# Shared weight buffers in the first group of an FFN's down product, a query rotation issued in pieces, an early output projection over two heads, and statistics and a gate chain queued later

## The chip, the core and the metric

The kernel runs on one core of a Trainium2 chip. A core has a matrix engine (TensorE, PE in the profile, with its weight loads shown apart as PEld), a vector engine (DVE), a scalar engine (ACT), GpSimd (POOL, here mostly a queue that issues transfers) and SyncE (SP, the queue that issues the weight loads). The metric is device time in microseconds, the median over runs.

## The reference

One decoder trunk on x (1024 positions, 1024 channels), all in fp32: a convolution layer, an FFN, an attention layer, an FFN and a last norm.

```python
h = h + short_conv_mixer(rms_norm(h, g))    # u = h @ w_in (1024 x 3072); b, c, val = split(u)
                                            # z = c * val; conv of width 3 over z; (b * conv) @ w_out
h = h + swiglu_ffn(rms_norm(h, g))          # g, u = split(h @ w13), 2 x 2816; (silu(g) * u) @ w2
c_lat, k_pe = ...                           # hn @ w_dkv: latent of 256, 64 rotated columns; k_nope, v = c_lat @ w_ukv
h = h + mla_mixer(rms_norm(h, g))           # query latent of 384, 8 heads of 128 + 64 rotated columns, causal softmax,
                                            # all heads with the same rotated key; then @ w_o (1024 x 1024)
h = h + swiglu_ffn(rms_norm(h, g))
return rms_norm(h, final_norm_g)
```

The rotation is `[x1*cos - x2*sin, x1*sin + x2*cos]` of the 64 rotated columns of a query head.

## The kernel before

Everything is held transposed: channels on the 128 partitions, the 1024 positions in the free dimension. Every fp32 operand of a product is split into a high and a low part (`split`, two instructions: ACT writes the high part at L92, DVE the low part at L93), and a product is three matmuls: high by high, high by low, low by high.

**Products by seven.** A product over pairs of blocks, two 128-row blocks of output by two halves of the positions, is done with seven products instead of eight (`pair`, L148 on, and `blocks`). For each it needs sums and differences of weight blocks (`sums`, L159 to L165, on DVE) and of operands (`mixed` in `operands`). The seven go in the order of `SEQ`. The results land in PSUM banks `ps_z` and `ps_y`, and a hook copies or adds them up. `raw_blocks` loads the four weight blocks of a pair of output rows into raw buffers named w11, w12, w22, w21 (pool `wraw`, ten buffers of 128x512), one more buffer holds the sums. The split weights go to five buffers `wo`.

**An FFN.** `up` runs over 22 blocks j of the inner width and leaves two at a time as the operands of one *pair* kp (11 pairs). `operands` builds seven split operands per pair (`xm`), which `move` (L85, POOL's queue) writes to memory (`md`), but for the last pair (kp 10), which stays on chip (`kept`). `back` then does the down product in groups of pairs given by `GROUPS`: in each group it runs over the four pairs of output rows, and adds to `h`. In the first group a pair is loaded with `load` after the third last `up`, the other after the last. While one group runs, the operands of the next are loaded. A group of kp 10, 2, 3 is not contiguous in the weights, so its four blocks take two transfers each.

**Attention.** For each head `scores` makes eight blocks of softmax (max at L946 on DVE, exponent at L949 on ACT), `pv` transposes them (`pt`) and multiplies by V; heads 0 to 5 go to memory (`od`), heads 6 and 7 stay on chip. `jobs` holds what is placed between: K and query of the next head, and, for two heads at once, the rotated query (`make_qr`) and V. `make_qr` rotates with `rope` (four DVE operations of 1024 positions), splits, and moves the eight quarters into place (`qrs`) on POOL's queue. In the last head the output projection of heads 0 and 1 (`project_o`, eight jobs) fills in; its operands (`oth`, `otl`) and the stream `h` come over POOL's queue.

**Convolution layer.** The first three products are done the plain way (`classic`), the rest by seven; `mix_x` queues the 16 mixed operands that these need. `gate_value` queues the gate chain (`scaled`, `taps`, `last`).

**What sets the order.** `queue` holds pieces of vector work that `drip` issues one at a time after each product. The text order is not the order on the engines: a list scheduler with a simulated timeline sets each engine's instruction order when the program is built, and the buffers of the pools are given out in the order of allocation. An instruction that writes a buffer waits for the last reader of what was there before.

Of the kernel before, what the change touches and what calls it, by code (L numbers as in the profile page):

```python
# [24 lines left out]
H = 8  # L25
# [11 lines left out]
EARLY = 2  # L37
GROUPS = ((0, 1), (10, 2, 3), (4, 5, 6), (7, 8, 9))
PREFETCH = 4
# [15 lines left out]
def trunk(ctx, tc, aps, out):  # L55
# [74 lines left out]
    def raw_blocks(w, kps, c1, c2):  # L130

        nk = len(kps)
        wv = w.rearrange("(k h p) n -> p h k n", p=P, h=2)
        R = {}
        for kh, c, key in ((0, c1, "11"), (0, c2, "12"), (1, c2, "22"), (1, c1, "21")):
            t = wraw("w" + key)
            i = 0
            while i < nk:
                n = 1
                while i + n < nk and kps[i + n] == kps[i] + n:  # L140
                    n += 1
                nc.sync.dma_start(t[:, i * P:(i + n) * P].rearrange("p (k m) -> p k m", m=P),
                                  wv[:, kh, kps[i]:kps[i] + n, c:c + P])
                i += n
            R[key] = t
        return R
# [332 lines left out]
    def back(w, load, st, final, ready, kept):  # L479
# [3 lines left out]
        for gi, g in enumerate(GROUPS):  # L483
            todo = []
            if gi + 1 < len(GROUPS):
                nxt = GROUPS[gi + 1]
                new = [{} for _ in nxt]
                if gi == 0:
                    new[0] = kept
                todo = [(i, kp, name) for name in SEQ for i, kp in enumerate(nxt) if gi or i]  # L490
            pace = -(-(NSLOT - KD - 2 - 7 * (len(g) + (gi == 0))) // 3)
# [43 lines left out]
    def next_operands(st, gain, spill=True):  # L535
# [3 lines left out]
        def final(mp):  # L539
            xs = []  # L540
            for n in (2 * mp, 2 * mp + 1):
                if spill:
                    move(hd[n], st[n])
                x = slot("xg")
                nc.scalar.activation(x, st[n], AF.Copy, scale=gcol(gain, n))
                xs.append(x)
            X.append({})
            operands(*xs, X[mp].__setitem__)
            for n in (2 * mp, 2 * mp + 1):
                queue.append(lambda n=n: stats(n, st[n]))  # L550
            if mp == KD // 2 - 1:
                drip()
        return X, final
# [7 lines left out]
    def first_product(w, c1, c2, emit):  # L561

        if run["n"] == 1:
            mix_x()
        if run["n"] < CLASSIC:
# [37 lines left out]
    def gate_value(j):  # L603
# [83 lines left out]
    def ffn(w13, w2, X, after, side=None):  # L687
# [35 lines left out]
        ready, kept = [{} for _ in GROUPS[0]], {}  # L723
        for j in range(KF):
            up(j)
            if j % 2:
                put = kept.__setitem__ if j == KF - 1 else lambda name, o, j=j: move(md[j // 2, SEQ.index(name)], o)
                operands(mid.pop(j - 1), mid.pop(j), put)
            if side:
                queue.append(lambda: next(side, None))  # L730
            if j == KF - 3:
                for name in SEQ:
# [34 lines left out]
    def rope(dst, src):  # L767

        t = slot("rt")
        nc.vector.tensor_tensor(t[0:64], src[64:128], sinT[64:128], ALU.mult)  # L770
# [59 lines left out]
    def rotated_keys():  # L830
        kr = slot("kr")
        rope(kr, kr0)
        nc.vector.tensor_tensor(kr, kr, get_R(), ALU.mult)
# [75 lines left out]
    def make_qr(h):  # L909
# [13 lines left out]
        nc.scalar.copy(out=q0, in_=ps)  # L923
        rope(qr, q0)
        yh, yl = slot("qrh", F32R), slot("qrl", F32R)
        split(yh, yl, qr)
        for a in range(2):
            t = slot("qrs", F32R)
            for i, y in enumerate((yh, yl)):
                for q in range(2):  # L930
                    r = i * 64 + q * 32
                    move(t[r:r + 32], y[q * 64 + a * 32:q * 64 + a * 32 + 32])
            Qt.setdefault(h + a, {})["r"] = t

# [57 lines left out]

    make_k(0)
    make_qr(0)
    make_q(0)
    make_v(0)
# [34 lines left out]
    for h in range(H):  # L1031
        if h >= 6:
            Od[h] = (slot("oth", F32R), slot("otl", F32R))
        if h + 1 < H:
# [9 lines left out]
        per = {2: ((0,), (1,), (), ()) if h == 0 else ((), (0,), (1,), ()), 4: ((0,), (1,), (2,), (3,)), 8: ((0, 1), (2, 3), (4, 5), (6, 7))}[len(jobs)]  # L1044
# [119 lines left out]
```

## Time and profile before

| | before |
| --- | --- |
| median of 3 runs | 2158.4 us (2157.68 to 2165.13) |
| profiled execution | 2161.49 us |
| its span | 2159.7 us |
| mean granted PE clock | 0.987 |
| PE busy | 2090.6 us, 97% |
| DVE busy | 1631.9 us, 76% |
| ACT busy | 938.7 us, 43% |
| DMA, mean rate | 149 GB/s |

How to read the rows below: a row of a timeline gives the start, the length, the engine, the line, the operation, output and input tiles, sizes, and in brackets the time the engine sat idle ahead of it and what ended that. A row of waits gives what waited, for what, the total in us, how many times, and the longest. A row of windows gives for one stretch the busy time of PE, PEld, DVE, ACT and POOL with the number of instructions, then the clock granted to PE, the DMA engines' busy share, and GB/s. In the stages of the kernel, the convolution layer runs to about 366 us, the first FFN to about 1000, attention from there to about 1490 with its heads between 1108 and 1440, and the second FFN to the end; `down` starts at about 790 and 1917.

### The profile page before, as it was taken

To read this page: it belongs to the slowest core of one execution; us is meant where nothing else is said; L and a number is where in the kernel's file an instruction comes from. 1 tells how busy PE (TensorE), PEld (TensorE's weight loads), DVE (VectorE), ACT (ScalarE), POOL (GpSimd) and SP (SyncE) were. 2 spreads that over 40 slices of the span, in tenths; PEclk is the share of its full clock that TensorE was granted. 3 is DMA by queue.
4 is the path that set the end of the run, shared out by engine and by line. 5 is a ranking of instruction groups with operands and counts; after the bars stand their busy time and mean duration, and the time that the engine had idled before them with its cause. 6 is when DMAs were issued, how large, how long until landed. Compare 5 with 4: busy or idle time off the path is not lost.

```text
span 2159.7 us, 27697 instructions
## 1 busy us (share of the span) xinstructions
PE 2090.6 (97%) x9798; PEld 1739.5 (81%) x9798; DVE 1631.9 (76%) x2694; ACT 938.7 (43%) x1729; POOL 244.0 (11%) x464
## 2 busy tenths in 40 slices
PE   8999999999999999999999999899999999999998
PEld 6788887888888877778888888787888888877886
DVE  5787757789988876689467777568888888876785
ACT  6533344444444443224345445345444444442235
POOL 1000100001101121110011112100001010121100
PEclk9999999999999999999999999999999999999998
DMA  6033462344545685865222213522435454685851
GB/s 242 25 98 119 143 206 93 122 142 129 183 130 177 206 286 195 272 214 163 51 57 60 55 42 85 199 80 78 132 122 176 145 162 147 192 275 195 282 190 78
DMA packets 267371, 321.29 MB, mean 149 GB/s; under 512 B 19855, under 2 KB 214608, under 8 KB 267232
## 3 DMA queue, kind: packets, MB, share of 16 engines
q0 software_dynamic: 61248, 201.46, 27.6%
q1 hardware_dynamic: 205984, 118.07, 18.5%
q8 instruction: 77, 1.26, 0.2%
q14 instruction: 62, 0.51, 0.1%
HBM read 206.22 MB, written 108.00 MB: 145 GB/s over the span
## 4 chain that ended last, share of the span: by engine, by line
PE 87%; DVE 6%; DMA 3%; ACT 2%; issue 2%; SPq 0%; POOL 0%; POOLq 0%; DVEq 0%; ACTq 0%
PE ps_z L184 36%; PE ps_y L184 27%; PE ps_c L229 6%; PE ps_s L943 3%; DMA w<-in_conv_ffn_w_dram 1%; PE ps_wo L105 1%; PE ps_wo L107 1%; PE ps_wo L109 1%; PE ps_l L109 1%; PE ps_l L105 1%; PE ps_l L107 1%; DMA w<-in_mla_ffn_w_dram 1%; PE ps_q L105 1%; PE ps_q L109 1%; PE ps_q L107 1%
## 5 line engine op out<-in xcount | busy, mean ns | idle before, releaser
L184 PE MATMUL ps_z<-x,wo 128*128 128x512 f32 x2532 | 612.6, 391 | 16.3 <-ACT z L198 6.9
L184 PEld LDWEIGHTS ps_z<-x,wo 128*128 128x128 f32 x2532 | 476.5, 189 | 118.7 <-ACT z L198 8.3
L184 PE MATMUL ps_y<-x,wo 128*128 128x512 f32 x1764 | 432.1, 390 | 1.2 <-DVE x L93 0.9
L184 PEld LDWEIGHTS ps_y<-x,wo 128*128 128x128 f32 x1764 | 330.8, 188 | 71.3 <-DVE x L93 2.1
L92 ACT CAST wo<-w 128x512 fp32r<-128x512 f32 (+2 forms) x423 | 239.4, 571 | 271.9 <-PE ps_y L184 109.2
L93 DVE TENSOR_TENSOR wo<-w,wo 128x512 fp32r<-128x512 f32 (+2 forms) x423 | 261.9, 625 | 58.7 <-ACT wo L92 58.1
L184 PE MATMUL ps_z<-xm,wo 128*128 128x512 f32 x960 | 242.9, 396 | 6.7 <-ACT wo L92 3.9
L184 PEld LDWEIGHTS ps_z<-xm,wo 128*128 128x128 f32 x960 | 181.5, 191 | 48.4 <-ACT wo L92 5.0
L92 ACT CAST wo<-sums 128x512 fp32r<-128x512 f32 (+2 forms) x172 | 98.7, 574 | 274.0 <-PE ps_y L184 102.1
L184 PE MATMUL ps_y<-xm,wo 128*128 128x512 f32 x720 | 185.2, 394 | 1.5 <-DVE h L504 1.3
L184 PEld LDWEIGHTS ps_y<-xm,wo 128*128 128x128 f32 x720 | 136.7, 191 | 32.4 <-DVE h L504 2.8
L85 POOL DMA_DIRECT2D md<-x x140 | 75.1, 537 | 740.0 <-DVE x L93 707.2
L198 ACT COPY z<-ps_z 128x512 f32<-128x512 f32 x106 | 62.2, 587 | 140.7 <-PE ps_z L184 140.5
L93 DVE TENSOR_TENSOR wo<-sums,wo 128x512 fp32r<-128x512 f32 (+2 forms) x172 | 107.9, 627 | 12.4 <-ACT wo L92 10.9
L504 DVE TENSOR_TENSOR h<-ps_z,h 128x512 f32<-128x512 f32 x104 | 71.7, 689 | 44.4 <-PE ps_z L184 43.6
L85 POOL DMA_DIRECT2D xm<-md x140 | 74.4, 538 | 266.9 <-PE ps_z L184 131.2
L93 DVE TENSOR_TENSOR x<-t,x 128x512 fp32r<-128x512 f32 x136 | 92.6, 689 | 3.3 <-ACT x L92 3.1
L238 DVE TENSOR_TENSOR a<-ps_y,z 128x512 f32<-128x512 f32 x88 | 60.8, 691 | 44.2 <-PE ps_y L184 43.9
L92 ACT CAST x<-t 128x512 fp32r<-128x512 f32 x136 | 83.0, 622 | 23.0 <-DVE t L253 20.1
L949 ACT ACTIVATE p<-ps_s,mx,qscale 128x128 f32<-128x128 f32 (+3 forms) x64 | 53.4, 836 | 79.9 <-DVE mx L947 79.9
L159 DVE TENSOR_TENSOR sums<-w,w 128x512 f32<-128x512 f32 (+2 forms) x85 | 53.4, 628 | 34.6 <-DMA w<-in_mla_ffn_w_dram 15.1
L504 DVE TENSOR_TENSOR h<-ps_y,h 128x512 f32<-128x512 f32 x88 | 60.5, 688 | 22.5 <-PE ps_y L184 22.4
(296 smaller groups left out, 3357.4 us busy)
## 6 DMA issues: line engine op xcount, KB each, us to landing
md<-x POOLq DMA_DIRECT2D x140, 512.0 KB, 3.7
xm<-md POOLq DMA_DIRECT2D x140, 512.0 KB, 8.4
w<-in_conv_ffn_w_dram SPq DMA_DIRECT2D x88, 256.0 KB, 2.9
w<-in_mla_ffn_w_dram SPq DMA_DIRECT2D x88, 256.0 KB, 3.0
w<-in_conv_w_in_dram SPq DMA_DIRECT2D x48, 256.0 KB, 2.9
hd<-h POOLq DMA_DIRECT2D x24, 512.0 KB, 3.6
hs<-hd SPq DMA_DIRECT2D x16, 512.0 KB, 12.0
yd<-yb POOLq DMA_DIRECT2D x12, 512.0 KB, 3.4
```

Source lines behind the costliest of these rows:

```text
L85: nc.gpsimd.dma_start(dst, src)
L92: nc.scalar.copy(out=hi, in_=src)
L93: (eng or nc.vector).tensor_tensor(lo, src, hi.bitcast(F32), ALU.subtract)
L105: nc.tensor.matmul(ps[:, hs], lhsT=wh, rhs=xh(k)[:, hs], start=st, stop=False)
L107: nc.tensor.matmul(ps[:, hs], lhsT=wh, rhs=xl(k)[:, hs], start=False, stop=False)
L109: nc.tensor.matmul(ps[:, hs], lhsT=wl, rhs=xh(k)[:, hs], start=False, stop=en)
L184: mm = lambda w_, x_, f: nc.tensor.matmul(b, lhsT=w_[:, m], rhs=x_, start=f, stop=True, skip_group_check=True)
L198: nc.scalar.copy(out=kept[name], in_=b)
L229: nc.tensor.matmul(ps[:, ts], lhsT=w_[:, m], rhs=X[i][f"b{kh}{th}"][:, q, :], start=st and j == 0, stop=en and j == 2)
L238: nc.vector.tensor_tensor(dst, ps, add, ALU.add)
L504: nc.vector.tensor_tensor(dst[name], b, dst[name], ALU.add)
L943: nc.tensor.matmul(ps[:, a:b], lhsT=q[:, qs], rhs=k[:, a:b], start=i == 0, stop=i == 4 and b < kw)
```

## The change

Five edits.

1. **Down's first group.** The groups of pairs are now (0, 1), (2, 3, 4), (5, 6, 7), (8, 9, 10). The pair kept on chip is kp 4, whose `up` blocks are computed last. Where a group has two pairs, w11 and w12 share one raw buffer, and so do w22 and w21. Every block is one transfer.
2. **The rotation** returns its four operations as pieces, which `make_qr` queues, followed by the split and the moves; one piece is issued after each block of scores.
3. **The early projection** is spread: three jobs in head 6 and five in head 7, at the places in `PLACES`. The operands of heads 0 and 1 and the first of `h` are loaded at the start of head 6.
4. **The gate chain**: `mix_x` is called after the first product of `gate_value(0)`, ahead of the chain of the first gate value in the queue.
5. **The statistics** of the last two blocks of `h` stay in the queue after the last operands of an FFN are issued.

```diff
-GROUPS = ((0, 1), (10, 2, 3), (4, 5, 6), (7, 8, 9))
+GROUPS = ((0, 1), (2, 3, 4), (5, 6, 7), (8, 9, 10))
+KEPT = 4
+PLACES = {0: ((0,), (1,), (), ()), 6: ((0,), (1,), (2, 3), (4,)), 7: ((0,), (1, 2), (3,), (4,))}
+PLACES.update({h: ((0,), (1,), (2,), (3,)) if h % 2 else ((), (0,), (1,), ()) for h in range(1, 6)})
@@ raw_blocks
-        for kh, c, key in ((0, c1, "11"), (0, c2, "12"), (1, c2, "22"), (1, c1, "21")):
-            t = wraw("w" + key)
-            i = 0
-            while i < nk:
...
-                nc.sync.dma_start(t[:, i * P:(i + n) * P].rearrange("p (k m) -> p k m", m=P),
-                                  wv[:, kh, kps[i]:kps[i] + n, c:c + P])
-                i += n
+        for q, (kh, c, key) in enumerate(((0, c1, "11"), (0, c2, "12"), (1, c2, "22"), (1, c1, "21"))):
+            if nk > 2 or q % 2 == 0:
+                t = wraw("w" + key)
+            else:
+                t = t[:, HS // 2:]
+            nc.sync.dma_start(t[:, :nk * P].rearrange("p (k m) -> p k m", m=P), wv[:, kh, kps[0]:kps[0] + nk, c:c + P])
@@ back
-                if gi == 0:
-                    new[0] = kept
-                todo = [(i, kp, name) for name in SEQ for i, kp in enumerate(nxt) if gi or i]
+                if KEPT in nxt:
+                    new[nxt.index(KEPT)] = kept
+                todo = [(i, kp, name) for name in SEQ for i, kp in enumerate(nxt) if kp != KEPT]
@@ next_operands
             if mp == KD // 2 - 1:
-                drip()
+                drip(len(queue) - 2)
@@ first_product
-        if run["n"] == 1:
-            mix_x()
@@ gate_value
         if j == 0:
+            mix_x()
             x_stats()
@@ ffn
-        for j in range(KF):
+        order = [k for kp in range(KF // 2) if kp != KEPT for k in (2 * kp, 2 * kp + 1)] + [2 * KEPT, 2 * KEPT + 1]
+        for j in order:
...
-            if j == KF - 3:
+            if j == order[-3]:
@@ rope
-        nc.vector.tensor_tensor(t[0:64], src[64:128], sinT[64:128], ALU.mult)
-        nc.vector.tensor_tensor(t[64:128], src[0:64], sinT[0:64], ALU.mult)
-        nc.vector.tensor_tensor(dst, src, cosT, ALU.mult)
-        nc.vector.tensor_tensor(dst, dst, t, ALU.add)
+        tt = nc.vector.tensor_tensor
+        return [lambda: tt(t[0:64], src[64:128], sinT[64:128], ALU.mult),
...
+                lambda: tt(dst, dst, t, ALU.add)]
@@ make_qr
-        rope(qr, q0)
+        def done():
...
+        queue.extend(rope(qr, q0))
+        queue.append(done)
@@ the loop over heads
-        else:
+        if h == H - 2:
             O0 = [load_o(k) for k in range(EARLY)]
-            for n in range(4):
+        if h == H - 1:
+            for n in range(3, 5):
                 h_of(n)
             O1 = [load_o(k) for k in range(EARLY, 6)] + [Od[6], Od[7]]
-            jobs = [lambda n=n: project_o(O0, 0, n) for n in range(KD)]
+        if h >= H - 2:
+            early = range(KD)[:3] if h == H - 2 else range(KD)[3:]
+            for n in early[:2]:
+                h_of(n)
+            jobs += [lambda n=n: project_o(O0, 0, n) for n in early]
+        per = PLACES[h]
         for i in range(4):
             pa, pb = p_tiles(i)
-            scores(Kt[h], Qt[h], 2 * i, pa)
-            scores(Kt[h], Qt[h], 2 * i + 1, pb)
+            if i == 0:
+                drip()
+            for qb, p in ((2 * i, pa), (2 * i + 1, pb)):
+                scores(Kt[h], Qt[h], qb, p)
+                drip(1)
```

What this does to the engines' order, at three places. First SP's queue, where the first FFN's `down` begins (w11 to w21 are raw buffers, a number for each allocation; `w2` is down's weight). Before:

```order
L142 DMA w11_6272<-in_conv_ffn_w2_dram 128x2x128
L142 DMA w12_6274<-in_conv_ffn_w2_dram 128x2x128
L142 DMA w22_6276<-in_conv_ffn_w2_dram 128x2x128
L142 DMA w21_6278<-in_conv_ffn_w2_dram 128x2x128
L142 DMA w11_6393<-in_conv_ffn_w2_dram 128x2x128
L142 DMA w12_6395<-in_conv_ffn_w2_dram 128x2x128
```

And now:

```order
L143 DMA w11_6272<-in_conv_ffn_w2_dram 128x2x128 x2
L143 DMA w22_6275<-in_conv_ffn_w2_dram 128x2x128 x2
L143 DMA w11_6391<-in_conv_ffn_w2_dram 128x2x128 x2
L143 DMA w22_6394<-in_conv_ffn_w2_dram 128x2x128 x2
L143 DMA w11_6492<-in_conv_ffn_w2_dram 128x2x128 x2
```

The same loads in the same order, into two allocations for a pair of output rows where there were four.

Second DVE in head 1, where the rotated query of heads 2 and 3 is made (`rt` and `qr` are the rotation, `mx` the maximum of a block of scores, `oh` and `pt` what PE waits for). Before:

```order
L770 TENSOR_TENSOR rt<-q_9227,sinT 64x1024
L771 TENSOR_TENSOR rt<-q_9227,sinT 64x1024
L772 TENSOR_TENSOR qr<-q_9227,cosT 128x1024
L946 TENSOR_REDUCE mx<-ps_s_9249 128x1
L93 TENSOR_TENSOR pt<-ps_t,pt 128x128
L946 TENSOR_REDUCE mx<-ps_s_9263 128x1
L773 TENSOR_TENSOR qr<-qr,rt 128x1024
L947 TENSOR_SCALAR mx<-mx,nqscale 128x1 x2
L93 TENSOR_TENSOR wqr<-wqr 128x2x2x32 x3
L93 TENSOR_TENSOR oh<-ps_pv,oh 128x256
L93 TENSOR_TENSOR qrl<-qr,qrh 128x1024
```

And now, first the two halves of `rt`, later in the head the rest:

```order
L770 TENSOR_TENSOR rt<-q_9203,sinT 64x1024
L771 TENSOR_TENSOR rt<-q_9203,sinT 64x1024
L954 RECIPROCAL rsum<-rsum 128x1
L950 TENSOR_REDUCE mx<-ps_s_9222 128x1
L955 TENSOR_SCALAR p<-p,rsum 128x384
L96 TENSOR_TENSOR oh<-ps_pv,oh 128x256
```

```order
L772 TENSOR_TENSOR qr<-q_9203,cosT 128x1024
L950 TENSOR_REDUCE mx<-ps_s 128x1
L954 RECIPROCAL rsum<-rsum 128x1
L773 TENSOR_TENSOR qr<-qr,rt 128x1024
L951 TENSOR_SCALAR mx<-mx,nqscale 128x1
L955 TENSOR_SCALAR p<-p,rsum 128x640
```

The product with the cosine and the sum now stand among the maxima of the fifth and sixth block of scores; the low half of the split (`qrl`) follows the maximum of the eighth.

Third POOL's queue at heads 6 and 7 (`od` takes the heads' output to memory, `oth` and `otl` bring it back, `h<-hd` loads the stream). Before:

```order
L85 DMA od<-oh 128x256 x10
L85 DMA oth<-od 128x1024
L85 DMA otl<-od 128x1024
L85 DMA oth<-od 128x1024
L85 DMA otl<-od 128x1024
L85 DMA h<-hd 128x1024 x4
L85 DMA oth<-od 128x1024
```

And now:

```order
L88 DMA od<-oh 128x256
L88 DMA oth<-od 128x1024
L88 DMA otl<-od 128x1024
L88 DMA oth<-od 128x1024
L88 DMA otl<-od 128x1024
L88 DMA h<-hd 128x1024 x2
L88 DMA od<-oh 128x256 x6
L88 DMA h<-hd 128x1024 x3
L88 DMA oth<-od 128x1024
```

The loads for the early projection and two blocks of `h` stand ahead of the last six moves of the heads' output.

More of the change, by code (lines that the diff above doesn't have):

```diff
@@ L134, in raw_blocks @@
         R = {}
-        for kh, c, key in ((0, c1, "11"), (0, c2, "12"), (1, c2, "22"), (1, c1, "21")):
-            t = wraw("w" + key)
-            i = 0
-            while i < nk:
[L139 to L142, printed above, removed]
-                                  wv[:, kh, kps[i]:kps[i] + n, c:c + P])
-                i += n
+        for q, (kh, c, key) in enumerate(((0, c1, "11"), (0, c2, "12"), (1, c2, "22"), (1, c1, "21"))):
[4 more added lines that the diff above has]
+            nc.sync.dma_start(t[:, :nk * P].rearrange("p (k m) -> p k m", m=P), wv[:, kh, kps[0]:kps[0] + nk, c:c + P])
             R[key] = t
@@ L723, in ffn @@
         ready, kept = [{} for _ in GROUPS[0]], {}
-        for j in range(KF):
+        order = [k for kp in range(KF // 2) if kp != KEPT for k in (2 * kp, 2 * kp + 1)] + [2 * KEPT, 2 * KEPT + 1]
+        for j in order:
             up(j)
             if j % 2:
-                put = kept.__setitem__ if j == KF - 1 else lambda name, o, j=j: move(md[j // 2, SEQ.index(name)], o)
+                put = kept.__setitem__ if j // 2 == KEPT else lambda name, o, j=j: move(md[j // 2, SEQ.index(name)], o)
                 operands(mid.pop(j - 1), mid.pop(j), put)
@@ L769, in rope @@
         t = slot("rt")
-        nc.vector.tensor_tensor(t[0:64], src[64:128], sinT[64:128], ALU.mult)
-        nc.vector.tensor_tensor(t[64:128], src[0:64], sinT[0:64], ALU.mult)
-        nc.vector.tensor_tensor(dst, src, cosT, ALU.mult)
-        nc.vector.tensor_tensor(dst, dst, t, ALU.add)
+        tt = nc.vector.tensor_tensor
+        return [lambda: tt(t[0:64], src[64:128], sinT[64:128], ALU.mult),
+                lambda: tt(t[64:128], src[0:64], sinT[0:64], ALU.mult),
+                lambda: tt(dst, src, cosT, ALU.mult),
+                lambda: tt(dst, dst, t, ALU.add)]
     w_dkv = A["w_dkv"].rearrange("(k p) n -> p k n", p=P)
@@ L831, in rotated_keys @@
         kr = slot("kr")
-        rope(kr, kr0)
+        for f in rope(kr, kr0):
+            f()
         nc.vector.tensor_tensor(kr, kr, get_R(), ALU.mult)
@@ L923, in make_qr @@
         nc.scalar.copy(out=q0, in_=ps)
-        rope(qr, q0)
[L925 to L933, printed above, removed]
+        def done():
+            yh, yl = slot("qrh", F32R), slot("qrl", F32R)
+            split(yh, yl, qr)
+            for a in range(2):
+                t = slot("qrs", F32R)
+                for i, y in enumerate((yh, yl)):
+                    for q in range(2):
+                        r = i * 64 + q * 32
+                        move(t[r:r + 32], y[q * 64 + a * 32:q * 64 + a * 32 + 32])
+                Qt.setdefault(h + a, {})["r"] = t
+        queue.extend(rope(qr, q0))
+        queue.append(done)
     def scores(K, Q, qb, p):
@@ L1033, in trunk @@
             Od[h] = (slot("oth", F32R), slot("otl", F32R))
+        jobs = []
         if h + 1 < H:
@@ L1037, in trunk @@
                 jobs = [lambda: make_qr(h + 1), lambda: make_v(h + 1)] + jobs
-        else:
+        if h == H - 2:
             O0 = [load_o(k) for k in range(EARLY)]
-            for n in range(4):
+        if h == H - 1:
+            for n in range(3, 5):
                 h_of(n)
             O1 = [load_o(k) for k in range(EARLY, 6)] + [Od[6], Od[7]]
-            jobs = [lambda n=n: project_o(O0, 0, n) for n in range(KD)]
-        per = {2: ((0,), (1,), (), ()) if h == 0 else ((), (0,), (1,), ()), 4: ((0,), (1,), (2,), (3,)), 8: ((0, 1), (2, 3), (4, 5), (6, 7))}[len(jobs)]
+        if h >= H - 2:
[4 more added lines that the diff above has]
+        per = PLACES[h]
         for i in range(4):
             pa, pb = p_tiles(i)
-            scores(Kt[h], Qt[h], 2 * i, pa)
-            scores(Kt[h], Qt[h], 2 * i + 1, pb)
+            if i == 0:
+                drip()
+            for qb, p in ((2 * i, pa), (2 * i + 1, pb)):
+                scores(Kt[h], Qt[h], qb, p)
+                drip(1)
             if len(pend) == DEPTH:
```

## The prediction

> **What bounds the kernel now.** I read the page's busy times and its chain by engine first, then PE's waits, then the windows in which they fall, then the timelines around the longest of them.
>
> ```profile
> PE 2090.6 (97%) x9798; PEld 1739.5 (81%) x9798; DVE 1631.9 (76%) x2694; ACT 938.7 (43%) x1729; POOL 244.0 (11%) x464
> PE 87%; DVE 6%; DMA 3%; ACT 2%; issue 2%; SPq 0%; POOL 0%; POOLq 0%; DVEq 0%; ACTq 0%
> ```
>
> PE is busy for 2090.6 of 2159.7 us and makes 87% of the chain that ended last. It is the bound, and the change adds and removes no matmul. So it can gain only PE's idle time (69.1 us) and matmuls that ran slowly. PE's waits, as total, times, longest:
>
> ```profile
> PE ps_z L184 <- DVE wo L93: 7.9, 4, 4.4
> PE ps_z L184 <- ACT z L198: 6.9, 3, 2.6
> PE ps_t L969 <- DVE oh L93: 4.6, 6, 1.2
> PE ps_z L184 <- ACT wo L92: 4.2, 3, 2.4
> ...
> PE ps_pv L981 <- ACT pt L92: 3.5, 1, 3.5
> ...
> PE ps_pv L981 <- DVE pt L93: 3.0, 3, 1.0
> PE ps_s L943 <- ACT p L949: 2.4, 2, 2.1
> PE ps_s L943 <- DVE h L1020: 2.1, 1, 2.1
> ```
>
> These eight are 34.6 us and are what the edits touch: `wo` is the split weight operand of a product (part A below), `oh` and `pt` with DVE stand in the heads that rotate a query (B), ACT `pt`, `p` and DVE `h` where the heads meet the output projection (C), `z` beside the gate chain and the changes of stage (D). The windows (PE, PEld, DVE, ACT, POOL busy; granted clock; DMA share; GB/s) price the rest of a gap:
>
> ```profile
> 756.00:810.00 54.00, 50.62 (x214) 40.50 (x213) 42.86 (x78) 25.26 (x50) 13.80 (x26) 0.97 0.84 286
> 810.00:864.00 54.00, 49.59 (x210) 40.53 (x209) 34.12 (x67) 17.73 (x37) 7.43 (x14) 0.94 0.60 195
> 1350.00:1404.00 54.00, 47.81 (x257) 41.33 (x258) 32.13 (x67) 18.04 (x41) 5.83 (x11) 0.91 0.55 198
> 1836.00:1890.00 54.00, 54.00 (x240) 44.72 (x239) 45.04 (x68) 24.96 (x42) 8.06 (x16) 1.00 0.60 190
> 1890.00:1944.00 54.00, 50.24 (x210) 39.87 (x209) 40.18 (x77) 24.83 (x52) 12.80 (x25) 0.97 0.81 275
> 1944.00:1998.00 54.00, 52.07 (x223) 42.59 (x222) 36.03 (x68) 15.90 (x32) 7.27 (x14) 0.97 0.60 195
> ```
>
> With no gap (1836 to 1890) a 512-column matmul takes 54.00/240 = 0.225 us at clock 1.00. Where there are gaps the clock is 0.91 to 0.97, and PE is slower while busy. So a gap has two prices: its idle time, and slow matmuls behind it.
>
> **A: down's first group.** The waits of the two FFNs where `down` begins (start, length, and in brackets the idle time before):
>
> ```profile
> 800.00 0.73 PE L184 MATMUL ps_z<-xm,wo 128*128 128x512 f32 x2 [2.35 <-ACT wo L92]
> ...
> 801.98 2.07 PE L184 MATMUL ps_z<-xm,wo 128*128 128x512 f32 x4 [0.78 <-DVE wo L93]
> ...
> 831.27 0.79 PE L184 MATMUL ps_z<-x,wo 128*128 128x512 f32 x1 [4.41 <-DVE wo L93]
> 831.86 2.76 PE L184 MATMUL ps_z<-xm,wo 128*128 128x512 f32 x6
> 1926.48 0.73 PE L184 MATMUL ps_z<-xm,wo 128*128 128x512 f32 x2 [1.58 <-ACT wo L92]
> ...
> 1928.46 2.07 PE L184 MATMUL ps_z<-xm,wo 128*128 128x512 f32 x4 [0.78 <-DVE wo L93]
> ...
> 1955.22 0.62 PE L184 MATMUL ps_z<-x,wo 128*128 128x512 f32 x1 [1.93 <-DVE wo L93]
> ```
>
> The engine named is the splitter, but the chain shows what it waited for: the raw weights, issued late.
>
> ```profile
> 787.91 8.88 DMA w<-in_conv_ffn_w_dram
> 821.09 8.92 DMA w<-in_conv_ffn_w_dram
> 778.01 0.37 SPq L142 DMA_DIRECT2D w<-in_conv_ffn_w_dram  x1
> 785.59 3.20 SPq L142 DMA_DIRECT2D w<-in_conv_ffn_w_dram  x3
> 799.52 0.37 SPq L142 DMA_DIRECT2D w<-in_conv_ffn_w_dram  x1
> ```
>
> A pair of output rows, in the first group 7 products of 2x3 matmuls (42×0.225 = 9.5 us), holds five of ten raw buffers before, three after. By the semaphores in the programs, SP's four loads for the second pair (PE takes it up at 800) wait before for the last `up` products to free buffers, from 785.6 to 799.5 in the trace. After, their buffers are freed with the first pair's, at about 778, 8 to 21 us earlier, so that even an 8.9 us landing ends by 787. The third pair's loads move to where the second's were, 799.5 at the latest against a need at about 810. The first pair of the second group, needed near 827 and landed at 830 (821.09+8.92), comes at least one pair earlier. Each was late once; none should be.
>
> Idle: 2.35+0.78+4.41 = 7.54 in the first FFN and 1.58+0.78+1.93 = 4.29 in the second, 11.8 together. Slow matmuls: 756 to 864 held 214+210 = 424 matmuls in 50.62+49.59 = 100.21 us, 4.8 over 424×0.225; 1890 to 1998 held 433 in 102.31, 4.9 over. Upper bound 11.8+9.7 = 21.5. The lower bound is 0: the buffers' data are no larger, DMA count falls by 16 in each FFN (one load per block in the second group instead of two), and the fourth pair kept instead of the last costs no transfer. I take **17**, the idle time and half of the slow part, since the windows also hold other small gaps. If this cover fails, what is late is the transfers of the moving operand:
>
> ```profile
> q0 software_dynamic: 1521, 5.53, 99.1%
> ...
> xm<-md POOLq DMA_DIRECT2D x10, 512.0 KB, 11.8
> w<-in_conv_ffn_w_dram SPq DMA_DIRECT2D x4, 128.0 KB, 8.3
> ```
>
> From 785 to 800 POOL's queue alone keeps the DMA engines at 99.1%: 5.53 MB in 15 us (0.37 MB a us), operands of 512 KB with 11.8 us to landing. Weights put among them make those later. A 128 KB load, 0.35 us at that rate, took 8.3 beside them, so the two queues share the engines.
>
> **B: query rotation in pieces.** Four 128-wide operations stood in a row on DVE ahead of the `oh` and `pt` which PE waited for:
>
> ```profile
> 1137.73 1.22 DVE L770 TENSOR_TENSOR rt<-q,sinT 64x1024 f32<-64x1024 f32 x1 [0.17 <-ACT q L923]
> 1164.83 1.23 DVE L946 TENSOR_REDUCE mx<-ps_s 128x1 f32<-128x1024 f32 x1 [1.44 <-PE ps_s L944]
> 1173.42 0.28 PE L943 MATMUL ps_s<-KH,qrs 128*128 128x128 f32 x1
> L85 POOL DMA_DIRECT2D qrs<-qrl x16: 499/499/522, 1102.2 to 1299.5; - x16
> DMA to landing us min/median/max: 2.2/3.1/4.5
> ```
>
> The order keeps two of them together and puts the last two (2×1.22 = 2.44) and the split (1.23) among later scores. The waits are 4.6+3.0 = 7.6 over three heads, 2.5 each, about what leaves. Upper bound 7.6; I take **5**. What is late next: the low half of the rotated query now stands behind the last score's maximum (1164.83). From there: 1.23 for it, 1.23 for the split (same width), 4×0.50 for POOL's moves and 3.1 to land give 1172.4, against the next head's first use at 1173.42: 1.0 us to spare, and 0.4 late with the longest landing, 4.5. The lower bound adds the high half's four moves (2.0) if all eight issue together: 2.4 late in each of three heads, −7.
>
> **C: early projection over two heads.** Head 6 ends in softmax waits with too little other work for PE, and head 7 had all eight projection jobs. Moving three of them forward fills the waits of 1350 to 1404: 2.4 (ACT p), 3.5 (ACT pt), 2.1 (DVE h), and a clock of 0.91, 54×0.09 = 4.9. Upper bound 12.9. I take **8**: the two ACT waits (5.9) and nearly half of the slow part; `h` is loaded and added in any case. The lower bound comes from POOL's queue, where a load of `h` waits in order for a free slot:
>
> ```profile
> POOL h L85 <- DVE pt L93: 20.8, 1, 20.8
> ```
>
> Two such loads now stand ahead of six `od` moves of the last heads.
>
> **D: gate chain and statistics.** Mixed operands now go ahead of the gate chain on DVE; the statistics of the last two h stay queued.
>
> ```profile
> 101.29 4.05 PE L184 MATMUL ps_z<-x,wo 128*128 128x512 f32 x10 [2.64 <-ACT z L198]
> 366.68 3.01 PE L184 MATMUL ps_z<-x,wo 128*128 128x512 f32 x12 [2.14 <-ACT z L198]
> 1491.63 4.39 PE L184 MATMUL ps_z<-x,wo 128*128 128x512 f32 x12 [2.15 <-ACT z L198]
> ```
>
> At 101.29: 2.64 idle and 4.05−10×0.225 = 1.8 slow, upper bound 4.4; I take **4**. Against it, the gate chain forms one burst behind; five split weights stand ready by then, so its lower bound is a wait as long as the one removed, −2.6. At 366.68 ACT's order is unchanged: 0. At 1491.63 one of two squares on ACT goes behind the first `z` copy; 2.15+(4.39−2.70) = 3.8 is the upper bound, nothing the lower; I take **1**, a quarter, since one of the two squares stays ahead.
>
> [...] The trace is divided: full rate after 2.14 at 366.68, but 0.37 a matmul after 2.15 at 1491.63 and 0.46 behind 4.41 at 831.86. [...]
>
> **Sum.** 17+5+8+4+1 = 35, and 2161.5−35 = 2126.5 on the profiled execution's own terms. That execution stood 3.1 above the median, 2158.4. I take the measured time between them and rather near the profiled one's, **2126**.
>
> **Rivals.**
> Operands in place of weights (0.15). Earlier weights share the full DMA stretch, and `xm` ends last. For: the 99.1%. Against: the loads of two pairs, 8×128 KB, are only 2.8 us at 0.37 MB a us. A falls from 17 to 5: 2126+12 = 2138.
> Rotated query late (0.10). For: 1.0 us to spare only. B turns from +5 to −7: also 2138.
> [...]
> POOL's queue jams in head 6 (0.06). The two `h` loads find no free slot and hold up the six `od` moves, on which `oth` for the projection rests. It decides once the slots come free later than the head's end. For: the 20.8 above. C's 8 is lost and two such waits come onto PE: 2126+8+2×20.8 = 2176, slower.
> The change does nothing measurable (0.04): buffers are freed no earlier because an earlier wait on the same queue holds SP. For: only one queue loads weights. Against: the releases named above. 2158.
> The forecast has the rest, 0.58.
>
> **Numbers.** All upper bounds (21.5+7.6+12.9+4.4+3.8 = 50.2) give 2111.3; A's idle time alone, nothing in B and half of C and D (11.8+4+2.5 = 18.3) give 2143.2. With the 3.1 by which executions differ put on at both ends, and rounded, the range is 2107 to 2147; it holds all cases but the jam and the null. No change is within 10.8 us of 2158.4 (0.5%, about what a measurement of this kernel can tell). Faster: 0.58+0.15+0.10+0.07 less 0.03 for their slow tails = 0.87; slower 0.06; same 0.07.
>
> **What would show it.** A: the waits on `wo` at both starts of `down` gone, the second pair's loads issued within 8 us of the first's, and clock 0.99 or more in the four windows. B: no waits of `ps_t` on `oh`, and `ps_s` of even heads not waiting for `qrs`. C: no gap over 1 us at the end of head 6, clock over 0.95 there, fewer project jobs in head 7. D: the 2.64 at 101 gone with nothing as long in the 20 us behind. The forecast is wrong if `xm` becomes the releaser at `down`, if POOL's `od` waits behind `h`, or if the gaps go and PE's busy time grows.

## The result, and the profile after

The changed kernel takes 2123.96 us (median of 4 runs, 2121.5 to 2124.29) against 2159.4 for the kernel before in the same comparison: a ratio of 0.9829, 95% interval 0.9809 to 0.9849. The forecast was 2126, from 2107 to 2147. Run again beside other kernels on another chip it took 2123.18 against 2160.62, a ratio of 0.9837 (0.9823 to 0.9852).

The page of the changed kernel, its engines and its chain by engine:

```profile
PE 2077.5 (98%) x9798; PEld 1730.1 (82%) x9798; DVE 1627.7 (77%) x2694; ACT 935.5 (44%) x1729; POOL 245.2 (12%) x464
PE 88%; DVE 6%; DMA 2%; ACT 2%; issue 2%; SPq 0%; POOL 0%; POOLq 0%; ACTq 0%; DVEq 0%
```

Every engine does the same number of instructions. PE's idle time (span less busy) fell from 69.1 to 2119.7−2077.5 = 42.2 us, 26.9 less, and its busy time fell by 13.1 with the same matmuls: both prices of a gap, as the prediction had them. That is one execution of each kernel, and they lie 40.0 us apart where the medians lie 35.4 apart. Of the waits that are left, these bear on the edits:

```profile
PE ps_s L947 <- ACT p L953: 3.1, 5, 1.6
...
PE ps_z L183 <- ACT z L197: 2.8, 3, 1.2
PE ps_y L183 <- DVE h L503: 2.0, 2, 1.8
...
PE ps_z L183 <- DVE wo L96: 1.6, 3, 0.8
PE ps_z L183 <- ACT wo L95: 1.6, 2, 1.3
...
PE ps_t L973 <- DVE oh L96: 1.1, 2, 0.6
```

DVE's `wo` went from 7.9 to 1.6, ACT's `z` from 6.9 to 2.8, ACT's `wo` from 4.2 to 1.6, DVE's `oh` from 4.6 to 1.1; the wait of 3.5 for ACT's `pt` and that of 2.1 of `ps_s` for `h` are gone. Two grew: `ps_y` for `h` from 1.3 to 2.0, nearly all of it one wait of 1.85, and `ps_s` for ACT's `p` from 2.4 to 3.1. Of the latter the 2.12 at the end of head 6 is gone; new are 1.55 in head 7 and 0.43 in each of heads 1, 3 and 5. The windows of the same stages (the first four begin 6 us earlier than before, or 30, the last is where head 6 ends):

```profile
750.00:804.00 54.00, 51.81 (x224) 41.25 (x223) 44.91 (x85) 26.79 (x54) 13.76 (x26) 1.00 0.85 293
804.00:858.00 54.00, 54.00 (x240) 44.72 (x239) 38.23 (x74) 18.34 (x38) 7.40 (x14) 1.00 0.59 195
...
1860.00:1914.00 54.00, 51.52 (x222) 41.03 (x221) 40.54 (x79) 26.90 (x58) 12.70 (x24) 1.00 0.84 284
1914.00:1968.00 54.00, 54.00 (x240) 44.72 (x239) 38.30 (x70) 15.27 (x31) 8.62 (x17) 1.00 0.64 210
1333.00:1387.00 54.00, 52.32 (x301) 44.98 (x300) 37.12 (x78) 22.99 (x53) 3.75 (x7) 1.00 0.45 152
```

The clock is 1.00 in all of them, and where `down`'s second group begins PE has no idle time (54.00 of 54.00). What is left stands at the start of `down`, at 793 in the first FFN and 1887 in the second, in the two changes of stage, in a small gap at 119, and at 1371 in head 7:

```profile
793.01 0.72 PE L183 MATMUL ps_z<-xm,wo 128*128 128x512 f32 x2 [1.32 <-ACT wo L95]
...
794.71 1.19 PE L183 MATMUL ps_z<-xm,wo 128*128 128x512 f32 x4 [0.51 <-DVE wo L96]
1887.71 1.66 PE L183 MATMUL ps_y<-xm,wo 128*128 128x512 f32 x6 [1.85 <-DVE h L503]
119.02 2.60 PE L183 MATMUL ps_z<-x,wo 128*128 128x512 f32 x10 [0.83 <-DVE wo L96]
360.66 3.01 PE L183 MATMUL ps_z<-x,wo 128*128 128x512 f32 x12 [1.19 <-ACT z L197]
1460.39 3.01 PE L183 MATMUL ps_z<-x,wo 128*128 128x512 f32 x12 [1.19 <-ACT z L197]
1370.82 0.73 PE L947 MATMUL ps_s<-kh,qnh 128*128 128x512 f32 x2 [1.55 <-ACT p L953]
```

### The profile page after: what moved, and what is told of

Same layout as the page of the kernel before. It is cut to its first block, busy times and chain, and to the rows that moved or that the text cites. A ratio compares the mean times of both kernels' runs of the same rounds, so it can differ in the third digit from the quotient of the medians.

```text
span 2119.7 us, 27634 instructions
## 1 busy us (share of the span) xinstructions
PE 2077.5 (98%) x9798; PEld 1730.1 (82%) x9798; DVE 1627.7 (77%) x2694; ACT 935.5 (44%) x1729; POOL 245.2 (12%) x464
## 4 chain that ended last, share of the span: by engine, by line
PE 88%; DVE 6%; DMA 2%; ACT 2%; issue 2%; SPq 0%; POOL 0%; POOLq 0%; ACTq 0%; DVEq 0%
PE ps_z L183 35%; PE ps_y L183 26%; PE ps_c L228 7%; PE ps_s L947 4%; PE ps_wo L108 1%; PE ps_wo L110 1%; PE ps_wo L112 1%; PE ps_l L112 1%; PE ps_l L108 1%; PE ps_l L110 1%; PE ps_pv L985 1%; PE ps_pv L986 1%; DMA w<-in_conv_ffn_w_dram 1%; PE ps_pv L987 1%; PE ps_q L108 1%
## 5 line engine op out<-in xcount | busy, mean ns | idle before, releaser
L158 DVE TENSOR_TENSOR sums<-w,w 128x512 f32<-128x512 f32 (+2 forms) x85 | 53.2, 626 | 29.4 <-DMA w<-in_mla_ffn_w_dram 13.4
```

Source lines behind the costliest of these rows:

```text
L158: tt(sums, R["12"], R["22"], ALU.add)
```

## The experiments

Read against the trace before, stage by stage (the same matmul's start in both), the 40 us between the two profiled executions came as 18.9 from A, 4 from B, 9 from C, 5.1 at the gate chain and 3.3 at the changes of stage. That was the theory of the first set: the parts as the prediction had them, by one execution each. Its rivals were that slow matmuls are not the gaps' doing, and that one part does another's work.

All of the runs, in three sets; a set ran on one chip and shares its runs of the kernel before:

| kernel | median us | range | ratio to before, 95% | PE idle, profiled us |
| --- | --- | --- | --- | --- |
| A alone | 2149.52 | 2142.5 to 2153.45 | 0.9942 (0.9923 to 0.996) | 54.9 |
| changed, B undone | 2132.37 | 2129.46 to 2133.97 | 0.9867 (0.985 to 0.9883) | 46.7 |
| changed, C undone | 2133.38 | 2131.22 to 2135.35 | 0.9873 (0.9856 to 0.9889) | 47.5 |
| changed, D undone | 2131.86 | 2131.05 to 2135.48 | 0.9871 (0.9852 to 0.989) | 45.7 |
| shared buffers alone | 2148.71 | 2144.7 to 2153.83 | 0.9943 (0.9926 to 0.996) | 57.6 |
| new groups alone | 2161.97 | 2150.96 to 2167.59 | 0.9993 (0.9976 to 1.0009) | 69.1 |
| changed, two sums buffers | 2120.41 | 2116.74 to 2122.55 | 0.981 (0.9793 to 0.9827) | 39.3 |
| changed, sums in halves | 2124.18 | 2120.77 to 2125.4 | 0.983 (0.9815 to 0.9846) | 40.2 |
| changed, again | 2123.18 | 2121.38 to 2124.99 | 0.9837 (0.9823 to 0.9852) | 41.5 |
| changed, A undone | 2138.8 | 2136.18 to 2143.05 | 0.9906 (0.989 to 0.9921) | 52.9 |
| B alone | 2157.21 | 2151.88 to 2166.52 | 0.9995 (0.9979 to 1.0011) | 63.7 |
| two sums, later statistics | 2117.22 | 2115.4 to 2119.1 | 0.9806 (0.9791 to 0.9821) | 37.8 |

The kernel before took 2160.1 in the first set (11 runs), 2162.93 in the second (17), 2160.62 in the third (17).

**A alone.** All edits of the first part on the kernel before: the groups, kp 4 kept, one transfer a block, and

```diff
-            t = wraw("w" + key)
+            if nk > 2 or q % 2 == 0:
+                t = wraw("w" + key)
+            else:
+                t = t[:, HS // 2:]
...
```

> Part A alone on the kernel before (shared raw buffers in down's first group, groups in order, kp 4 kept). Theory from the two traces (stage by stage, A is worth 11.2 us from 800 to 1087 in the first FFN and 7.7 in the second): 18.9 less, 2140.5, with the 4.41 gap gone, the first gap in the first FFN near 1.3 instead of 2.35, and heads, gate chain and changes of stage as before. Rival, that only idle time comes with A and the slow matmuls have another cause: 11.2 less, 2148. Rival, that the parts help each other and A alone is worth much less: above 2150.

Its profiled execution was 2142.5 us, close to the theory's 2140.5, but the median of its six is 2149.52, 10.6 below before. By the ratio A alone is worth 0.58%, 12.5 us (8.6 to 16.6). Idle time fell by 14.2. The spread of the executions, 11 us with the clock from 0.986 to 0.989, says that one profiled execution prices the slow part badly; the 18.9 was too much.

**A undone** in the changed kernel, and the changed kernel again beside it:

> The changed kernel with down's first group as before (four buffers a pair, groups with kp 10, two transfers a block there). A alone gave 10.6 on the kernel before. Theory, that the parts add and that A is worth its idle time (11.2 in the traces): 2134 to 2136. The prediction's 17 would give 2141, the 18.9 of the two profiled executions 2143.

> The changed kernel once more, as the measure for the others of this set on the same chip: 2124 and a ratio to before of 0.983. What each theory says of it: its executions lie closer together than those of the kernel before (which spread over 10 us), if slow matmuls come by chance behind gaps, since it has fewer gaps.

Undoing A costs 2138.8−2123.18 = 15.6 us, between the two theories. Idle time rose by 52.9−41.5 = 11.4. So A is worth its 11 to 14 us of idle time and about 4 of slow matmuls at most, 10.6 to 15.6 in all; not 18.9. As expected the changed kernel's executions lie close together (3.6 us in five; the kernel before 12.8, in seventeen).

**What in A does it.** First only the sharing, with the groups and their transfers as before:

```diff
-            t = wraw("w" + key)
+            t = wraw("w" + key) if nk > 2 or q % 2 == 0 else t[:, HS // 2:]
```

> On the kernel before, only the sharing of raw buffers in down's first group; groups stay (0, 1), (10, 2, 3) and so on, with two transfers a block in the second. Theory, that the gain of A is loads released earlier by fewer buffers: nearly all of A, 2141 to 2144, the 4.41 gap gone. Rival, that the second group's first gap comes from its eight transfers instead of four on the weight queue: the 4.41 gap stays, 2150.

Then only the groups, with four buffers a pair:

```diff
-GROUPS = ((0, 1), (10, 2, 3), (4, 5, 6), (7, 8, 9))
+GROUPS = ((0, 1), (2, 3, 4), (5, 6, 7), (8, 9, 10))
+KEPT = 4
...
```

> On the kernel before, only the new groups and kp 4 kept, one transfer a block, with four raw buffers a pair as before. Theory: the loads are released as late as before, so 2155 to 2159, gaps at the first pairs as before (2.35, 0.78) and at the second group at most 1 us shorter. Rival, that the number of transfers sets the gap: the 4.41 goes, 2149.

Sharing alone has the ratio of A alone (0.9943 and 0.9942), and PE has no gap there at the second group. The groups alone have 0.9993, and the gap at the second group stays, in both FFNs, with half as many transfers:

```profile
833.79 1.20 PE L185 MATMUL ps_y<-xm,wo 128*128 128x512 f32 x4 [3.40 <-DVE wo L94]
...
1962.81 1.65 PE L185 MATMUL ps_y<-xm,wo 128*128 128x512 f32 x3 [6.57 <-DVE wo L94]
```

So the gain is the earlier release, and the number of transfers counts for nothing that can be measured. The change's regrouping gives nothing by itself.

**What still waits at the start of down.** The rows on DVE, first of the kernel before, then of the changed one (L159 and L158 are the first sum of a pair of rows, L162 and L161 its second):

```profile
796.89 0.43 DVE L159 TENSOR_TENSOR sums<-w,w 128x256 f32<-128x256 f32 x1 [2.25 <-DMA w<-in_conv_ffn_w_dram]
...
799.03 0.42 DVE L162 TENSOR_TENSOR sums<-sums,w 128x256 f32<-128x256 f32 x1
```

```profile
788.42 0.42 DVE L158 TENSOR_TENSOR sums<-w,w 128x256 f32<-128x256 f32 x1 [0.95 <-DMA w<-in_conv_ffn_w_dram]
...
791.77 0.42 DVE L161 TENSOR_TENSOR sums<-sums,w 128x256 f32<-128x256 f32 x1
```

By the semaphores of the two programs, the sum that waits for a transfer is not that of the pair which PE is at. Before it belongs to the third pair of rows, whose load was issued at 787.91 when the first pair's buffer came free, and took 8.88 us; behind it in DVE's order stands L162, the second pair's, from which the split for PE's matmul at 800.00 is made. In the changed kernel it is the fourth pair's:

```profile
779.64 8.69 DMA w<-in_conv_ffn_w_dram
```

The third pair's loads are early now, the fourth's stand where the third's were. To test it, two versions of the changed kernel let ten buffers hold all four pairs of the first group, so that the fourth pair's loads wait for the last `up` product. In the one, the third and fourth pair's sums take the buffers of the first and second pair, which also puts the sums late in DVE's order:

```diff
+    spare = []
...
-        sums = wraw("sums")[:, :n]
+        if nk > 2:
+            spare.clear()
+            sums = wraw("sums")[:, :n]
+        else:
+            spare.append(wraw("sums") if len(spare) < 2 else spare[len(spare) - 2])
+            sums = spare[-1][:, :n]
```

> The changed kernel with the sums of the third and fourth pair of rows of the first group in the buffers of the first and second, so that ten buffers hold all four pairs: the fourth pair's loads wait for the last up product instead of the first pair, and its sum stands on DVE behind the second pair's sixth product. Theory from the trace after: what PE still waits for at 793 (1.32 and 0.51) and at 1887 (1.85) is a product whose split stands on DVE behind the sum of a later pair, which waits for that pair's load (8.69 us to land). Then these gaps go: 1.8 in the first FFN and 2 in the second, 4 to 6 with the slow part: 2118 to 2120. Rival, that DVE has too much work there: the gaps stay within 0.5, 2123 to 2124.

In the other, the sums of two pairs share the halves of one buffer, and a sum may stand early:

```diff
+    spare = {}
...
-        sums = wraw("sums")[:, :n]
+        if nk > 2:
+            sums = wraw("sums")[:, :n]
+        elif "s" in spare:
+            sums = spare.pop("s")[:, HS // 2:]
+        else:
+            spare["s"] = wraw("sums")
+            sums = spare["s"][:, :n]
```

> The changed kernel with the sums of two pairs of rows in the two halves of one buffer: the loads of the fourth pair are issued as early as with two buffers reused, but its sum is free to stand early, and stands four vector instructions behind the one that releases its load. If DVE's order is what costs: DVE stands there for the rest of the load (3 to 9 us from issue), and the gap is as large as in the changed kernel or larger, 2124 to 2130. If the time of the load's issue is what costs: gaps gone, 2118 to 2120.

The two starts of `down`, with two buffers reused and then with halves:

```profile
789.72 0.73 PE L190 MATMUL ps_z<-xm,wo 128*128 128x512 f32 x2 [0.24 <-ACT wo L95]
...
1883.22 1.65 PE L190 MATMUL ps_y<-xm,wo 128*128 128x512 f32 x6 [0.23 <-DVE h L510]
```

```profile
791.25 0.74 PE L191 MATMUL ps_z<-xm,wo 128*128 128x512 f32 x2 [0.24 <-ACT wo L95]
...
1885.64 1.65 PE L191 MATMUL ps_y<-xm,wo 128*128 128x512 f32 x6 [0.19 <-DVE h L511]
768.83 0.43 DVE L166 TENSOR_TENSOR sums<-w,w 128x256 f32<-128x256 f32 x1 [0.98 <-DMA w<-in_conv_ffn_w_dram]
```

The gap in the second FFN went from 1.85 (1.79 in the other execution of the changed kernel) to 0.23 and 0.19, and that in the first from 1.32 (but 0.28 in the other execution) to 0.24. With halves a sum stood early and waited for a transfer, but only 0.98: the load had gone out at 766.6 and took 2.1 us, while the DMA engines moved 257 GB/s (760 to 768); the changed kernel issues it at 779.6, where they move 412 GB/s (776 to 784), and there it took 8.69. So, by the traces, it is the late issue of a later pair's load that costs, seen by PE through DVE's order; an early place in that order costs little while the loads are early. In time the one version gives 2120.41, just over its expectation and with an interval that overlaps the changed kernel's, the other 2124.18, no gain: its idle time fell by only 1 to 2 us, and by the medians no gain from taking these gaps away is shown.

**B undone** in the changed kernel, and **B alone** on the kernel before. The edit in `make_qr`, undone:

```diff
-        queue.extend(rope(qr, q0))
-        queue.append(done)
+        for f in rope(qr, q0):
+            f()
+        done()
```

> The changed kernel with the query rotation, its split and its moves issued at once again. Theory: the three heads that rotate get their DVE waits back, 1.3 us a head pair, 4 in all: 2128. The prediction's 5 would give 2129. Rival, that heads gain by the early projection alone: 2124, no change of the head period (73.9 us a pair of heads).

> The query rotation in pieces alone, on the kernel before. Theory from the stages of the trace: 1.3 us of idle time for each of three rotating heads, 4, so a ratio of 0.998; if the slow matmuls behind those gaps count as well, as the 8.4 of the undoing says, 0.996. The prediction's 5: 0.9977. Rival, that the rotated query comes late: 1.00 or more, with a wait at the first use of it in the next head.

Undone, the DVE waits of the rotating heads are back as before (the rows are those of head 1):

```profile
1130.50 0.33 PE L974 MATMUL ps_t<-ident,p 128*128 128x128 f32 x1 [1.20 <-DVE oh L96]
...
1133.65 0.58 PE L986 MATMUL ps_pv<-pt,vh 128*128 128x256 f32 x1 [1.00 <-DVE pt L96]
```

In the changed kernel each of these heads has one short wait in their place, and the wait on `oh` in the even heads, which was there before, stays:

```profile
1139.22 0.68 PE L947 MATMUL ps_s<-kh,qnh 128*128 128x512 f32 x2 [0.43 <-ACT p L953]
...
1164.90 0.33 PE L973 MATMUL ps_t<-ident,p 128*128 128x128 f32 x1 [0.56 <-DVE oh L96]
```

Idle time says 4.5 to 5.4 both ways (46.7 against 42.2 and 41.5; 69.1 against 63.7 alone). The time says 0.0030 of 2160, 6.5 us, by the ratios when undone, and 0.0005 with an interval of ±0.0016 alone, which is no measurable change. The first agrees with the idle time within what the two ratios leave open, about 5 us; the second, at most 0.0021 or 4.5 us, only with its lower end. So B is worth its 4 to 5 us by the idle time, and not shown by time alone. In the profiled execution of the undoing PE's clock was at 0.50 for 10.2 us behind gaps of two rotating heads, but also for 6.8 us at the changes of stage, which this edit leaves alone:

```profile
1132.50:1139.33 6.83, 5.83 (x29) 5.68 (x27) 5.20 (x10) 3.68 (x9) 3.01 (x7) 0.50 0.63 159
...
1470.42:1473.83 3.41, 3.41 (x9) 2.63 (x10) 3.41 (x5) 2.29 (x4) 0.00 (x0) 0.50 0.01 2
```

The rival of a late rotated query is out: no wait for it stands in any even head, with B alone or in the changed kernel.

**C undone**: all eight jobs in the last head again, with the loads there.

```diff
-PLACES = {0: ((0,), (1,), (), ()), 6: ((0,), (1,), (2, 3), (4,)), 7: ((0,), (1, 2), (3,), (4,))}
+PLACES = {0: ((0,), (1,), (), ()), 6: ((), (0,), (1,), ()), 7: ((0, 1), (2, 3), (4, 5), (6, 7))}
...
-        if h == H - 2:
+        if h == H - 1:
             O0 = [load_o(k) for k in range(EARLY)]
-        if h == H - 1:
-            for n in range(3, 5):
+            for n in range(4):
                 h_of(n)
...
-        if h >= H - 2:
...
+            jobs = [lambda n=n: project_o(O0, 0, n) for n in range(KD)]
```

> The changed kernel with all eight early projection jobs in the last head and their loads there. Theory: the waits of 3.5 and 2.1 us at the end of head 6 and the slow clock there come back, 9 us: 2133, with a clock near 0.91 in the 54 us around the start of head 7. Rival, that the loads of the operands at the start of head 6 cost elsewhere what they gain: below 2128.

2133.38 is where the theory had it (2133). The three waits are back where the heads change, with the clock at 0.94 in the window:

```profile
1328.75 0.74 PE L947 MATMUL ps_s<-kh,qnh 128*128 128x512 f32 x2 [2.17 <-ACT p L953]
1336.31 0.55 PE L985 MATMUL ps_pv<-pt,vh 128*128 128x256 f32 x1 [3.46 <-ACT pt L95]
1375.53 0.64 PE L947 MATMUL ps_s<-kh,qnh 128*128 128x512 f32 x2 [2.20 <-DVE h L1025]
1322.00:1376.00 54.00, 45.94 (x256) 39.91 (x255) 32.17 (x68) 18.77 (x44) 11.95 (x22) 0.94 0.65 225
```

By the ratios C is worth 0.0036, 7.8 us, and by the medians of the two sets 10. In the changed kernel the third of these places, in head 7, keeps the 1.55 on ACT's `p`, so of its three waits, 7.8 us, 6.3 go.

**D undone**: `mix_x` behind the gate chain, all statistics issued with the last operands.

```diff
+        if run["n"] == 1:
+            mix_x()
...
-            mix_x()
             x_stats()
...
-                drip(len(queue) - 2)
+                drip()
```

> The changed kernel with the mixed operands queued behind the gate chain again and all statistics issued with the last operands. Theory from the traces: 5.1 us at the gate chain (2.64 idle and slow matmuls) and 0.95 and 2.4 at the two changes of stage come back, 8.4: 2132. The prediction's own terms, 4 and 1: 2129. Rival, that a slow stretch behind a gap is chance: only 2.6+0.95+0.95 = 4.5 comes back, 2128.5, and the matmuls behind the gaps run at 0.23 us.

2131.86, as the theory had it (2132): 0.0034 by the ratios, 7.3 us. The gaps are back, two of the three with slow matmuls behind them:

```profile
100.24 4.06 PE L183 MATMUL ps_z<-x,wo 128*128 128x512 f32 x10 [2.63 <-ACT z L197]
...
365.55 4.61 PE L183 MATMUL ps_z<-x,wo 128*128 128x512 f32 x12 [2.13 <-ACT z L197]
...
1466.94 3.01 PE L183 MATMUL ps_z<-x,wo 128*128 128x512 f32 x12 [2.13 <-ACT z L197]
```

By the ratios the four undoings add up to 0.0069+0.0030+0.0036+0.0034 = 0.0169, against 0.0163 for the whole change. Each of these prices is open by about 5 us, and those of B, C and D compare runs of two chips, so the idle time says it better: against the changed kernel run again the four undoings cost 11.4+5.2+6.0+4.2 = 26.8 of the 69.1−41.5 = 27.6 that the whole change gains. The parts add.

**A version that beats both.** The two sums buffers, and the last two squares held back further:

```diff
                 drip(len(queue) - 2)
+                queue.extendleft([lambda: None] * 3)
```

> The changed kernel with the sums of the first group's third and fourth pair in the buffers of the first and second, and the last two squares of the statistics held back three products more. Theory: the two waits of 1.19 at the changes of stage (a square ahead of the copy that PE waits for) go as well, 2.4 less than the kernel with the two sums, and with them the slow matmuls that follow some of them: 2116 to 2119. Rival, that another piece of work then stands ahead of that copy: no gain, 2120.

2117.22, 2115.4 to 2119.1 in four runs, against 2121.38 to 2124.99 for the changed kernel on the same chip: 6 us less than the change, with ranges that don't meet, and the 95% intervals of the ratios just miss each other (0.9821 and 0.9823). Neither change of stage waits for a `z` copy any more; only the small gap ahead of it is left:

```profile
1456.47 0.73 PE L190 MATMUL ps_y<-x,wo 128*128 128x512 f32 x2 [0.47 <-DVE x L96]
```

Against the two sums alone (2120.41, another set) the gain of 3 is about what the two waits of 1.19 would give, but lies within the intervals.

## Why the prediction was right

2126 was forecast and 2123.96 measured, by the mechanism forecast: gaps in which PE waited. By terms, predicted and measured by undoing, where each time is open by about 5 us:

| term | predicted us | measured us (by ratio) | idle time alone |
| --- | --- | --- | --- |
| A | 17 | 14.9, and 12.5 alone | 11.4 to 14.2 |
| B | 5 | 6.5, and 1.1 alone | 4.5 to 5.4 |
| C | 8 | 7.8 | 5.3 to 6.0 |
| D | 5 | 7.3 | 3.5 to 4.2 |
| sum | 35 | 35.2 for the whole | 26.9 |

**A** may have been a little too large (the forecast of 17 lies just outside the 8.6 to 16.6 of A alone), and its story was half right. "Earlier release of the loads" holds, as the sharing alone shows, and the 4.41 and 1.93 gaps at the second group went whole. The step that failed is "SP's four loads for the second pair (PE takes it up at 800) wait before for the last `up` products": the second pair's loads had gone out by then, and the load that PE waited for at 800 was the third pair's, through a sum that stood in DVE's order ahead of the second pair's. So "each was late once; none should be" was wrong too: the fourth pair's load takes the same place, and 3.7 us of idle time (1.32+0.51+1.85) stayed there in the profiled execution. The lateness moved from the third pair to the fourth. The sign named for A, no waits on `wo` at either start of `down`, did not come: 3.2 us of them are left.

**B** went as reckoned. The order put the last two operations and the split later, and the waits on `oh` and `pt` in the rotating heads went. The bound of 7.6 was too large: three of the six waits on `oh`, 1.7 us, stand in the even heads of the kernel before, where no query is rotated, and two of them, 1.1, are what is left. Of the other 5.9, three new waits of 0.43 on ACT's `p` take back 1.3, which leaves 4.6. The margin at the next head was larger than the 1.0 us reckoned: the first use of the new query at 1155.67 had no wait.

**C** went as reckoned in both ACT waits and the clock. Two of its sums were off, without harm to the term: the wait of 2.14 for `h`, left out of the 8, gave way to one of 1.55 on ACT's `p` at the same place in head 7, and the slow part of 4.9 in the bound counted idle time a second time, since of the 10.24 us in which the clock was at 0.50 PE was busy for only 6.79, so an estimated half of that, 3.4, is slow (at the same 0.50 a matmul took 0.46 at 831.86, against 0.225 with no gap; the kernel before):

```profile
1351.29:1361.53 10.24, 6.79 (x28) 6.00 (x27) 4.57 (x12) 2.86 (x7) 3.56 (x7) 0.50 1.08 420
1361.53:1364.95 3.42, 3.42 (x23) 3.02 (x23) 2.28 (x7) 2.11 (x5) 0.00 (x0) 1.00 1.13 420
```

POOL's queue did not jam; its waits for a free slot in head 7 (`h` on PE's `ps_pv`: 24.6 us in three, the longest 13.2) stayed off the path, where POOL has 0%.

**D** was too small by the traces, in two places; by time its 5 and the 7.3 cannot be told apart. At the second change of stage a quarter of the bound was taken, because one square stays ahead; the whole slow part went in that execution. And "at 366.68 ACT's order is unchanged: 0" was a misreading of the order: there too one square goes behind the first `z` copy, as the trace shows, with 2.14 down to 1.19:

```profile
359.08 1.05 ACT L296 ACTIVATE sq<-h 128x1024 f32<-128x1024 f32 x1
360.04 0.56 ACT L197 COPY z<-ps_z 128x512 f32<-128x512 f32 x1
360.51 1.06 ACT L296 ACTIVATE sq<-h 128x1024 f32<-128x1024 f32 x1
```

The predicted wait in the gate chain's burst, the lower bound there, came as the small gap at 119: 0.83.

**The rivals.** Operands in place of weights: `xm` never became the releaser, though the load's 8.69 us in the full stretch is what is left of it. The rotated query was not late, POOL's queue was not jammed, and the change does what it says. That slow matmuls are no consequence of these gaps has 0.07 in the sum of the chances, a number that no run shows; idle time alone (A 11.8, B 5, C 5.9, D 3.1, together 25.8) would have given 2161.5−25.8 = 2135.7. In place of that number the runs showed slow matmuls behind some gaps and not behind others, as counted below; the whole change brought 13.1 us of busy time in the profiled executions, and 2124, so it falls as a whole. That the total came within 2 us is in part luck: the slow part differs from execution to execution, half of it was taken for A and for C without a reason that fixes the half, and A's too much and D's too little, as far as they can be told, cancelled.

## What to carry to other kernels

When an engine waits for a transfer, ask the program whose transfer it is: an engine can stand, in its own order, at work of a later step that a scheduler put ahead (here DVE, 2.25 us ahead of the third pair's sum at 796.89), and then the buffers of that later step are what to free. Price an edit by the idle time it removes first; the slow matmuls behind gaps change from execution to execution, so one profiled execution of a kernel can overstate or understate them by several microseconds (for A here 18.9 against 10.6 to 15.6). And read an order row by row before a term is set to zero.

## What the runs showed of the hardware

In these runs a gap in PE's work was followed not always by matmuls at little more than half speed (0.38 and 0.46 us each in the two examples below), and more often the longer it was. The fourteen profiled executions share a few gaps, each with 7 to 12 matmuls of 512 columns behind it, which take 0.25 to 0.27 us each where nothing slows them:

| gap, us | where | followed by slow matmuls (0.35 us or more each) |
| --- | --- | --- |
| 0.82 to 0.83 | 117 to 119, after the gate chain | 0 of 8 |
| 1.19 | both changes of stage | 3 of 14 |
| 2.13 to 2.15 | both changes of stage | 8 of 12 |
| 2.63 to 2.64 | 101, at the gate chain | 6 of 6 |

Two examples, the first from the changed kernel run again (whose first execution had 3.01 behind the same gap of 1.19), the second from the kernel with sharing alone, where the matmuls took 0.46 each:

```profile
1458.26 4.60 PE L183 MATMUL ps_z<-x,wo 128*128 128x512 f32 x12 [1.19 <-ACT z L197]
```

```profile
1485.55 5.49 PE L184 MATMUL ps_z<-x,wo 128*128 128x512 f32 x12 [2.13 <-ACT z L198]
```

The same gap gives 3.01 in one execution and 4.60 in the next: gaps of 1.19 were followed by slow matmuls in 3 of 14 cases, and all six of 2.63 to 2.64.

The granted clock shows how long slow stretches lasted. In the profiled execution of the kernel before the clock was at 0.50 in seven stretches between 50 and 2090 us, five of 3.41 us, one of 6.83 and one of 10.24. In the 3.41 us ahead of each PE was idle for 1.93 to 2.64 us. Less was enough in the changed kernel run again, where the gap of 1.19 at the second change of stage has one of 0.47 just ahead of it: behind 3.41−1.75 = 1.66 us of idle time the clock fell to 0.50:

```profile
1455.75:1459.16 3.41, 1.75 (x7) 1.07 (x7) 3.41 (x6) 3.41 (x6) 0.00 (x0) 1.00 0.43 130
1459.16:1462.58 3.42, 3.42 (x10) 2.64 (x9) 3.42 (x5) 1.52 (x4) 0.00 (x0) 0.50 0.06 14
```

In its first execution the idle time around the same two gaps was as large, 0.76+0.90 in the two rows, and the clock stayed at 1.00:

```profile
1456.08:1459.49 3.41, 2.65 (x10) 1.34 (x8) 3.41 (x6) 3.41 (x7) 0.00 (x0) 1.00 0.89 237
1459.49:1462.91 3.42, 2.52 (x11) 2.10 (x12) 3.42 (x6) 3.33 (x6) 0.00 (x0) 1.00 0.01 2
```

This may also be why the kernel before spreads over 13 us in its runs (2151.18 to 2164.01 in one set, with the clock from 0.984 to 0.989) and the changed one over 4: it has more gaps, and its clock was longer at 0.50 (by the traces 34.1 us between 50 and 2090 us before, none and 3.4 in the two executions of the changed kernel). That is the author's estimate. A run with a lower clock is broadly a longer one in every set (in that one 2151.18 at 0.989 and 2164.01 at 0.984). Why the same idle time was followed by a slow stretch in one execution and not in the other is left open.
